# A router with stationary weights in four column groups, and attention's weighted values for two query blocks at once

## The chip, the cores and the metric

One core of a Trainium2 chip (trn2) runs one program. The metric is device time in microseconds (us) of one execution. The engines are TensorE (PE in the profile, its weight loads PEld), VectorE (DVE), ScalarE (ACT), GpSimd (POOL) and SyncE (SP, which here issues DMA transfers). Each engine works through its own instructions in order.

## The reference

An encoder of two layers on 512 tokens of 1024 values, float32. In each layer four mixers (Hyena, Mamba2, attention and HGRN2) work on 256 columns each, and an expert mixture follows. The change touches the weighting of values in attention (4 heads of 64) and the router.

```python
for l in range(DEPTH):                       # 2 layers
    hn = rmsnorm(x, norm_mix_w[l])
    proj = hn @ w_in[l]                      # columns for the four mixers
    ...
    x = x + concat([ya, yb, yc, yd]) @ w_out[l]
    x = x + expert_choice_moe(rmsnorm(x, norm_ffn_w[l]), ...)

def expert_choice_moe(x, w_router, w_gate, w_up, w_down):
    cap = EC_CAPACITY * L // N_EXPERTS       # 64 tokens for each of 16 experts
    aff = softmax(x @ w_router)              # 512 x 16
    gate, idx = top_k(swapaxes(aff, 1, 2), cap)
    xe = x[idx]
    hdn = silu(xe @ w_gate) * (xe @ w_up)
    ye = (hdn @ w_down) * gate
    ...
```

Attention's three bands come together in one table of biases that is added to the logits, so that the kernel makes, for each head, a softmax over 512 keys and the product with v.

## The kernel before, in words

A layer runs in stages: HGRN2, Mamba2, Hyena, attention, each woven with projections; then the router, then 16 experts. `weave` draws pieces from several streams by given shares and so fixes the order in which instructions are written. A framework keeps each engine's instructions in an order of its own making, close to it, and puts in the semaphores; the expert part keeps the order as written. Tiles come from pools of a fixed number of slots: N (9 slots), B (13), G (9 pages of 2 KB a partition, `page`), H (12) and others. A load into a slot waits until the slot's last reader is done.

Attention (`attn`) goes over two pairs of heads (i), four blocks of 128 queries (b) and the two heads of a pair (h). `logits` makes a 128x512 block of logits on PE (`alog`), adds the table and takes the maximum on DVE (L970), and the exponential and its sum on ACT (L973). `turn` follows three steps later: four PE transposes (`apT`), copied half by DVE (L982) and half by ACT (L983) into the page `aPT`. After the second head `weigh` multiplies with the values (`apv`, L990): for each of four key chunks and both heads a product into 64 of 128 partitions and 128 columns. After the last block of a pair `factors` and `values` scale it into `ars`, and it is split into a high and a low part (`mxh`, `mxl`) for the output projection. Attention is woven with that projection's other parts (`out_part`, tiles `po`, L1220 to L1222, each time three matmuls of 512 columns, added to x by DVE). A float32 matmul appears in the trace as two records for one instruction, a transpose as one.

The router (`router`) goes over four tiles of 128 tokens: eight transposes (`rxT`), copied by DVE and ACT (`rx`, L1273 and L1275), and eight matmuls `rl` (L1278) with a block of `rx` stationary (128x128) and 16 columns of the router's weights `rw` moving. DVE takes the maximum (L1280), ACT the sum of squares of the tile (`junk`, L1284, and `ssffn`) and the exponential (L1289). Then expert 0's affinities are laid out as rows (`er`), ranked on DVE (L1301), its tokens picked by matmuls (`ex`, L1335), transposed (`exT`), and the expert's three products follow (`eg`, `eu`, `ey`, L1399).

The experts' weights (`we`, L1391, 512 KB for a chunk of 128x1024) are loaded by SP into a ring of slots of the pools, as far ahead as slots come free. In attention and the router SP works through the loads for the first experts; behind them stand loads into slots that the experts themselves give back.

Of the kernel before, what the change touches and what calls it, by code (L numbers as in the profile page):

```python
# [15 lines left out]
AF = mybir.ActivationFunctionType  # L16
# [4 lines left out]
P = 128  # L21
# [3 lines left out]
NE = 16  # L25
# [7 lines left out]
R_NMIX, R_HCW, R_MCW, R_MCB, R_MNW, R_LB, R_HGN, R_FRQ, R_B1, R_B2, R_NFFN, R_N = (  # L33
    0, 8, 26, 46, 50, 52, 60, 61, 62, 63, 64, 72)

C_ID, C_LE, C_GE, C_IOTA, C_TOK, C_HALF, C_KEY, C_SLOT, C_N = 0, 128, 256, 384, 448, 452, 453, 455, 456


def shape_constants():
    f32 = np.float32  # L40
    p = np.arange(P)
    c = np.zeros((P, C_N), f32)
    c[:, C_ID:C_ID + P] = np.eye(P)
    c[:, C_LE:C_LE + P] = p[:, None] <= p[None, :]
    c[:, C_GE:C_GE + P] = p[:, None] >= p[None, :]
    c[:, C_IOTA:C_IOTA + 64] = np.arange(1, 65)
    c[:, C_TOK:C_TOK + 4] = 2 * (P * np.arange(4)[None, :] + p[:, None])
    c[:, C_HALF] = p >= 64
    c[:, C_KEY] = 1.0 / KEY
    c[:, C_KEY + 1] = 1.0  # L50
    c[:, C_SLOT] = p % 64 + 1
    same = (p[:, None] // 32) == (p[None, :] // 32)
    m = np.zeros((P, 2, P), np.int32)
    m[:, 0] = same & (p[:, None] <= p[None, :])
    m[:, 1] = same & (p[:, None] >= p[None, :])

    eo = np.concatenate([np.arange(0, L, 2), np.arange(1, L, 2)])
    f = 2.0 * np.pi * (np.arange(P, dtype=np.float64) + 0.5) / (2 * L)  # L60
    n = np.arange(L).reshape(P, 4).T
    th = n[:, :, None] * f
    dft = np.stack([np.cos(th), np.sin(th)]).astype(f32)
    idft = np.ascontiguousarray(dft.transpose(0, 1, 3, 2))
    tk = [eo[:, None] * f, eo[:, None] * (np.pi / 2 - f)]
    kdft = np.stack([np.concatenate([np.cos(tk[0]), np.cos(tk[1])], axis=1),
                     np.concatenate([np.sin(tk[0]), -np.sin(tk[1])], axis=1)])
    kdft = (kdft * (2.0 / (2 * L))).astype(f32)

    t = np.linspace(0.0, 1.0, L, dtype=f32)[:, None]  # L70
    ang_pos = (f32(2.0 * math.pi) * np.arange(L, dtype=f32) / f32(L)).astype(f32)
    bands = np.linspace(1e-4, 15, 16, dtype=f32)
    ang = (ang_pos[:, None] * bands[None, :]).astype(f32)
    z = np.concatenate([t, np.cos(ang), -np.sin(ang)], axis=-1).astype(f32)
    lo = math.log(1e-2) / 1.5
    hi = math.log(1e-2) / 0.3
    deltas = np.abs(np.linspace(lo, hi, 256, dtype=f32))
    decay = np.exp(-t * deltas[None, :]).astype(f32)[eo]

    d = np.arange(511, -512, -1)  # L80
    n = np.abs(d)
    nf = np.maximum(n, 1).astype(f32)
    large = 8 + (np.log(nf / f32(8)) / f32(math.log(128.0)) * f32(8)).astype(np.int32)
    bucket = (d > 0) * 16 + np.where(n < 8, n, np.minimum(large, 15))
    mult = (n <= 64).astype(int) + ((n <= 256) & (n % 4 == 0)) + (n % 16 == 0)
    oh = np.zeros((33, 1024), f32)
    oh[bucket, np.arange(1023)] = 1.0
    oh[32, :1023] = np.where(mult > 0, np.log(np.maximum(mult, 1)), -1e30)
    return {
        "c_pack": c, "c_hmask": m, "c_dft": dft, "c_idft": idft, "c_kdft": kdft,  # L90
        "c_zT": np.ascontiguousarray(z.T), "c_decay": decay, "c_bucket": oh,
    }
# [18 lines left out]
def encoder(ctx: ExitStack, tc: tile.TileContext, d, out, dbg=None, stages=None, nlayers=NL):  # L111
    nc = tc.nc
    V, A, G, T, SY = nc.vector, nc.scalar, nc.gpsimd, nc.tensor, nc.sync
# [24 lines left out]
    def tl(tag, shape, name, dt=F32):  # L138
        return tagged(pools[tag], tag, shape, dt, name)

    def small(shape, name, dt=F32, bufs=1):
        return tagged(sm, "s_" + name, shape, dt, name, bufs=bufs)
# [4 lines left out]
    def bank_b(name):  # L147
        return tagged(psb, "b", [512], F32, name)

    def page(shape, name, dt=F32):  # L150
        return tl("G", shape, name, dt)
# [52 lines left out]
    pk = cp.tile([P, C_N], F32, name="pk")  # L204
# [11 lines left out]
    def xrow(t):  # L216
        return X[t]
# [735 lines left out]
    def attn(l, st, scr, ahead=3):  # L953
        q, k, v = st
        mix_tile(2)
        tab, den, PT, po = {}, {}, {}, {}

        def logits(i, b, h):
            if b == 0 and h == 0:
                tab[i] = [tl("B", [896], "atab") for _ in range(2)]  # L960
                for g in range(2):
                    SY.dma_start(tab[i][g], bass.AP(tensor=scr.tensor, offset=scr.offset + (2 * i + g) * 1024,
                                                    ap=[[1, P], [1, 896]]))
                den[i] = small([4, 2], "aden", bufs=2)
            ps = bank_b("alog")
            for m in range(2):
                T.matmul(ps, q[i][:, h, b * P:(b + 1) * P], k[i][m][:, h], start=(m == 0), stop=(m == 1))
            lg = page([L], "alg")
            mx = small([1], "amx", bufs=4)
            V.tensor_tensor_reduce(lg, ps, tab[i][h][:, 128 * b:128 * b + 512][:, ::-1], 1.0, -3e38,  # L970
                                   ALU.add, ALU.max, mx)
            V.tensor_scalar(mx, mx, -1.0, None, op0=ALU.mult)
            A.activation(lg, lg, AF.Exp, bias=mx, accum_out=den[i][:, b, h:h + 1])  # L973
            return lg

        def turn(i, b, h, lg):
            pt = bank_b("apT")
            for c in range(4):
                T.transpose(pt[:, c * P:(c + 1) * P], lg[:, c * P:(c + 1) * P], ident)
            PT[h] = page([4, P], "aPT")  # L980
            src = pt.rearrange("p (c q) -> p c q", c=4)
            V.tensor_copy(PT[h][:, 0:2], src[:, 0:2])  # L982
            A.activation(PT[h][:, 2:4], src[:, 2:4], AF.Copy)  # L983

        def weigh(i, b):
            if b == 0:
                po[i] = bank_a("apv")
            for c in range(4):
                for g in range(2):
                    T.matmul(po[i][64 * g:64 * g + 64, b * P:(b + 1) * P],  # L990
                             v[:, c, (2 * i + g) * 64:(2 * i + g + 1) * 64], PT[g][:, c],
                             start=(c == 0), stop=(c == 3))

        def factors(i):
            V.reciprocal(den[i], den[i])
            dn = page([4, 2, 64], "adn")
            V.tensor_copy(dn, den[i][:, :, :, None].to_broadcast([P, 4, 2, 64]))
            pr = bank_b("aden")
            for b in range(4):
                T.transpose(pr[:, b * P:(b + 1) * P], dn[:, b].rearrange("p h c -> p (h c)"), ident)  # L1000
            rs = page([L], "ars")
            A.activation(rs, pr, AF.Copy)
            return rs

        def values(i, rs):
            V.tensor_mul(rs, rs, po[i])
            mix_put(2, i, rs)

        todo = [(i, b, h) for i in range(2) for b in range(4) for h in range(2)]
        lgs = {}  # L1010
        for n in range(len(todo) + ahead):
            if n < len(todo):
                lgs[n] = logits(*todo[n])
            m = n - ahead
            if m >= 0:
                turn(*todo[m], lgs.pop(m))
                end = todo[m][1:] == (3, 1)
                if end:
                    rs = factors(todo[m][0])
                if todo[m][2]:  # L1020
                    weigh(*todo[m][:2])
                if end:
                    values(todo[m][0], rs)
            yield 2
# [229 lines left out]
    def router(rw, st, xd):  # L1254


        pl = bank_b("rl")
        plv = pl[:, :64].rearrange("p (t e) -> p t e", t=4)
        rt = tl("H", [D], "ra")
        ra = rt[:, :12 * NE].rearrange("p (t e c) -> p t e c", t=4, e=NE)  # L1260
        mx = small([4], "rmx")
        den = small([4], "rden")
        V.tensor_copy(ra[:, :, :, 2], pk[:, C_TOK:C_TOK + 4, None].to_broadcast([P, 4, NE]))
        for t in range(4):
            xs = []
            for h in range(2):
                ps = bank_b("rxT")
                for k in range(4):
                    T.transpose(ps[:, k * P:(k + 1) * P], xrow(t)[:, (4 * h + k) * P:(4 * h + k + 1) * P], ident)
                xT = page([4, P], "rx")  # L1270
                src = ps.rearrange("p (k c) -> p k c", k=4)
                if not h:
                    V.tensor_copy(xT, src)  # L1273
                else:
                    A.activation(xT, src, AF.Copy)  # L1275
                xs.append(xT)
            for k in range(8):
                T.matmul(plv[:, t], xs[k // 4][:, k % 4], rw[:, k], start=(k == 0), stop=(k == 7))  # L1278
            af, r = ra[:, t, :, 0], ra[:, t, 0, 1:2]
            V.reduce_max(mx[:, t:t + 1], plv[:, t], axis=AX.X)  # L1280
            V.tensor_scalar(af, plv[:, t], mx[:, t:t + 1], None, op0=ALU.subtract)
# [353 lines left out]
```

## Time and profile before

| | us |
|---|---|
| runs of the kernel | 1667.71, 1661.7, 1661.99 (median 1661.99) |
| the profiled execution's own time | 1665.74 |
| its span in the trace | 1664.0 |
| TensorE busy in the span | 1536.9 (92%) |
| VectorE | 805.7 (48%) |
| ScalarE | 396.1 (24%) |
| moved by DMA | 468.55 MB, 282 GB/s over the span |

The span is from the first to the last instruction of the trace. A busy share is an average over stages: in the experts' stages TensorE and the DMA are both nearly always busy, in the mixers only TensorE. What bounds a stage has to be read in that stage.

### The profile page before, as it was taken

What the parts mean: (1) busy time and instruction counts of PE and PEld (TensorE: products, weight loads), DVE (VectorE), ACT (ScalarE), POOL (GpSimd) and SP (SyncE); (2) the same over time, 40 slices, a digit from 0 to 9 for tenths busy, and PEclk for the clock granted to TensorE, in tenths of its full rate; (3) what the DMA queues carried; (4) which work ended last, traced back from release to release, by engine and by line L of the source; (5) the groups of instructions that cost most, each with busy time, mean ns of one, the idle gap of its engine ahead of it and who ended that gap; (6) DMA issues with size and microseconds to landing.
All of it is one profiled execution on the core that took longest, in us unless ns stands there. A gap on an engine that the chain in (4) does not pass through costs nothing.

```text
span 1664.0 us, 22783 instructions
## 1 busy us (share of the span) xinstructions
PE 1536.9 (92%) x8899; PEld 879.6 (53%) x8899; DVE 805.7 (48%) x1727; ACT 396.1 (24%) x805; POOL 214.0 (13%) x214
## 2 busy tenths in 40 slices
PE   7989999989999998998889999999899999999985
PEld 6778788763433433332368788787534433332332
DVE  6777777562433342331266767856533433332323
ACT  4344434430001010000152435243200001000012
POOL 3232132000000000000033232300000000000001
PEclk9989999989999999999989889999899999999998
DMA  5411224679999999999912202167799999999995
GB/s 165 129 51 28 75 76 162 237 265 369 421 419 422 420 421 420 420 422 420 385 54 80 74 26 77 55 231 261 256 402 419 420 421 420 421 420 420 420 421 239
DMA packets 153486, 468.55 MB, mean 282 GB/s; under 512 B 20408, under 2 KB 56664, under 8 KB 144418
## 3 DMA queue, kind: packets, MB, share of 16 engines
q1 hardware_dynamic: 144742, 455.10, 69.8%
q0 software_dynamic: 2240, 7.34, 1.1%
q10 hardware_dynamic: 6396, 4.65, 0.8%
q8 instruction: 70, 1.15, 0.3%
q14 instruction: 38, 0.31, 0.0%
HBM read 460.60 MB, written 6.44 MB: 281 GB/s over the span
## 4 chain that ended last, share of the span: by engine, by line
PE 61%; DMA 25%; DVE 6%; ACT 3%; issue 2%; POOL 2%; ACTq 0%; SPq 0%; DVEq 0%; POOLq 0%
DMA we<-in_moe_w_up_dram 10%; PE eg L1399 9%; DMA we<-in_moe_w_down_dram 7%; PE eu L1399 7%; PE ey L1399 7%; DMA we<-in_moe_w_gate_dram 6%; PE pcm L395 3%; PE pcm L396 3%; PE pcm L397 3%; PE ec L1470 3%; PE po L1220 2%; PE po L1221 2%; PE po L1222 2%; PE ptm L418 2%; PE ptm L417 2%
## 5 line engine op out<-in xcount | busy, mean ns | idle before, releaser
L1399 PE MATMUL eu<-we,exT 128*64 128x512 f32 x1024 | 239.4, 599 | 20.3 <-DMA we<-in_moe_w_up_dram 18.4
L1399 PE MATMUL ey<-we,ehT 128*64 128x512 f32 x1024 | 232.9, 598 | 18.8 <-ACT ehT L1435 11.5
L1399 PE MATMUL eg<-we,exT 128*64 128x512 f32 x1024 | 231.2, 597 | 10.6 <-DMA we<-in_moe_w_gate_dram 5.9
L1399 PEld LDWEIGHTS eu<-we,exT 128*64 128x64 f32 x1024 | 67.0, 136 | 187.2 <-issue 87.9
L1301 DVE SCALAR_TENSOR_TENSOR ra<-er,ra,tie 128x512 bf16<-128x512 f32 x128 | 95.9, 749 | 135.4 <-PE er L1309 132.5
L1399 PEld LDWEIGHTS ey<-we,ehT 128*64 128x64 f32 x1024 | 69.0, 136 | 157.9 <-issue 96.3
L1399 PEld LDWEIGHTS eg<-we,exT 128*64 128x64 f32 x1024 | 68.8, 136 | 151.4 <-issue 107.3
L1452 DVE SCALAR_TENSOR_TENSOR eY<-ey,erg,eY 64x512 fp32r<-64x512 f32 x64 | 48.0, 749 | 205.3 <-ACT eY L1451 205.2
L1420 ACT ACTIVATE eh<-eg 128x512 f32<-128x512 f32 x32 | 19.1, 598 | 505.3 <-PE eg L1399 505.3
L397 PE MATMUL pcm<-hT,whl 128*128 128x512 f32 x320 | 128.9, 403 | 3.5 <-DVE whl L381 3.5
L396 PE MATMUL pcm<-hT,whl 128*128 128x512 f32 x320 | 130.3, 407 | 0.0
L395 PE MATMUL pcm<-hT,whl 128*128 128x512 f32 x320 | 130.1, 406 | 0.0
L1471 DVE TENSOR_TENSOR x<-x,ec 128x512 f32<-128x512 f32 x128 | 79.8, 682 | 102.8 <-PE ec L1470 102.8
L1346 POOL DMA_INDIRECT exe<-xd,erow x28 | 27.8, 994 | 783.2 <-DVE erg L1327 526.6
L1451 ACT ACTIVATE eY<-ey,erg 64x512 fp32r<-64x512 f32 x64 | 43.7, 683 | 269.4 <-PE ey L1399 245.0
L1427 DVE TENSOR_TENSOR eh<-eh,eu 128x512 f32<-128x512 f32 x32 | 22.0, 688 | 158.7 <-PE eu L1399 158.7
L417 PE MATMUL ptm<-wtm,hT 128*128 128x256 f32 (+1 forms) x256 | 76.5, 300 | 1.7 <-DVE aqs L924 1.7
L1470 PE MATMUL ec<-eY,eot 128*128 128x512 f32 x256 | 67.3, 405 | 10.2 <-DVE erow L1344 6.4
L418 PE MATMUL ptm<-wtm,hT 128*128 128x256 f32 (+1 forms) x256 | 74.6, 293 | 1.3 <-DVE wtm L381 1.3
L380 POOL TENSOR_SCALAR whl<-wraw 128x1024 fp32r<-128x1024 f32 x40 | 46.7, 1169 | 222.1 <-PE pcm L397 113.8
L419 PE MATMUL ptm<-wtm,hT 128*128 128x256 f32 (+1 forms) x256 | 73.7, 291 | 0.0
L397 PEld LDWEIGHTS pcm<-hT,whl 128*128 128x128 f32 x320 | 62.4, 195 | 18.3 <-DVE whl L381 3.9
(386 smaller groups left out, 2381.4 us busy)
## 6 DMA issues: line engine op xcount, KB each, us to landing
we<-in_moe_w_gate_dram SPq DMA_DIRECT2D x216, 512.0 KB
we<-in_moe_w_up_dram SPq DMA_DIRECT2D x208, 512.0 KB
we<-in_moe_w_down_dram SPq DMA_DIRECT2D x204, 512.0 KB
wraw<-in_w_in_dram SPq DMA_DIRECT2D x27, 1024.0 KB
we<-in_moe_w_down_dram SPq DMA_DIRECT2D x26, 1024.0 KB
we<-in_moe_w_up_dram SPq DMA_DIRECT2D x24, 1024.0 KB
we<-in_moe_w_gate_dram SPq DMA_DIRECT2D x20, 1024.0 KB
wo<-in_w_out_dram SPq DMA_DIRECT2D x8, 1024.0 KB
```

Source lines behind the costliest of these rows:

```text
L380: G.tensor_scalar(dst_hi, raw, 1.0, 0.0, op0=ALU.mult, op1=ALU.add)
L395: T.matmul(ps, w[:, 0, k, :], H[k], start=(k == 0), stop=False)
L396: T.matmul(ps, w[:, 0, k, :], Lo[k], start=False, stop=False)
L397: T.matmul(ps, w[:, 1, k, :], H[k], start=False, stop=(k == 7))
L417: T.matmul(dst, h, w[:, 0, k % 4], start=(k == 0), stop=False)
L418: T.matmul(dst, h, w[:, 1, k % 4], start=False, stop=False)
L419: T.matmul(dst, g, w[:, 0, k % 4], start=False, stop=(k == 7))
L1301: V.scalar_tensor_tensor(g, pr, ra[:, c, e, 0:1], tie[:, 384 - c * P:896 - c * P], op0=ALU.subtract, op1=ALU.is_gt, accum_out=k)
L1399: T.matmul(ps[f][64 * f:64 * f + 64], xT[:, j, h], qs[4 * h + j][:, f * 512:(f + 1) * 512], start=(h == 0 and j == 0), stop=(h == 1 and j ...
L1452: V.scalar_tensor_tensor(lo, src, w[c, 0:1], hi.bitcast(F32), op0=ALU.mult, op1=ALU.subtract)
L1470: T.matmul(ps, ot[:, t * P:(t + 1) * P], Y[i][q][n], start=(q == 0), stop=(q == 1))
L1471: V.tensor_add(xrow(t)[:, c], xrow(t)[:, c], ps)
```

## The change

Attention: the tile `aPT` now holds a head's transposed weights for two blocks of queries (4 chunks x 2 blocks x 128) and comes from pool N, where it came from the page pool for one block. `weigh` runs after every second block, with 256 moving columns where it had 128, so half as many instructions.

Router: the weights are padded with zeros to eight blocks of 128x32 (`rp`, in the tile `ra`) and are now the stationary side; the tokens (`rx`, 128 columns) move. Block k writes into the 32 output partitions of its column group k mod 4 (`rc`, L1285), so that four partial sums stand one below the other. DVE copies them to SBUF (`rpart`, L1288), and one matmul with a 0/1 matrix of 128x16 from the constants (`C_SUM`) as the moving side adds the four groups and gives the logits (`rl`, L1289). A PSUM bank more is used.

```diff
@@ shape_constants
+    c[:, C_SUM:C_SUM + NE] = (p % 32)[:, None] == np.arange(NE)
...
@@ attn
-            PT[h] = page([4, P], "aPT")
+            if b % 2 == 0:
+                PT[h] = tl("N", [4, 2, P], "aPT")
             src = pt.rearrange("p (c q) -> p c q", c=4)
-            V.tensor_copy(PT[h][:, 0:2], src[:, 0:2])
-            A.activation(PT[h][:, 2:4], src[:, 2:4], AF.Copy)
+            V.tensor_copy(PT[h][:, 0:2, b % 2], src[:, 0:2])
+            A.activation(PT[h][:, 2:4, b % 2], src[:, 2:4], AF.Copy)
 
         def weigh(i, b):
-            if b == 0:
+            if b == 1:
                 po[i] = bank_a("apv")
             for c in range(4):
                 for g in range(2):
-                    T.matmul(po[i][64 * g:64 * g + 64, b * P:(b + 1) * P],
-                             v[:, c, (2 * i + g) * 64:(2 * i + g + 1) * 64], PT[g][:, c],
+                    T.matmul(po[i][64 * g:64 * g + 64, (b - 1) * P:(b + 1) * P],
+                             v[:, c, (2 * i + g) * 64:(2 * i + g + 1) * 64], PT[g][:, c].rearrange("p b q -> p (b q)"),
                              start=(c == 0), stop=(c == 3))
...
-                if todo[m][2]:
+                if todo[m][1] % 2 and todo[m][2]:
                     weigh(*todo[m][:2])
...
@@ router
-        pl = bank_b("rl")
+        pc, pl = bank_b("rc"), bank_b("rl")
...
+        rp = rt[:, 768:].rearrange("p (k c) -> p k c", k=8)
+        V.memset(rp, 0.0)
+        V.tensor_copy(rp[:, :, :NE], rw)
...
             for k in range(8):
-                T.matmul(plv[:, t], xs[k // 4][:, k % 4], rw[:, k], start=(k == 0), stop=(k == 7))
+                q = k % 4
+                T.matmul(pc[32 * q:32 * q + 32, t * P:(t + 1) * P], rp[:, k], xs[k // 4][:, k % 4],
+                         start=(k < 4), stop=(k >= 4))
+            part = page([P], "rpart")
+            V.tensor_copy(part, pc[:, t * P:(t + 1) * P])
+            T.matmul(plv[:, t], part, pk[:, C_SUM:C_SUM + NE], start=True, stop=True)
```

The order of instructions differs in attention and the router of each layer. On TensorE, at layer 0's first weighing of values in attention, before (a name's number tells one tile from another; `aks` and `aqs` are keys and queries, `av` the values, `wos` the projection's weights):

```order
L967 MATMUL alog_2744<-aks_2414,aqs_2336 128x512
L990 MATMUL apv_2721<-aPT_2702,av_2481 64x128
L1220 MATMUL po_2730<-wos_2639,mxh_2179 128x512
L1221 MATMUL po_2730<-wos_2639,mxh_2179 128x512
L1222 MATMUL po_2730<-wos_2639,mxl_2180 128x512
L1220 MATMUL po_2730<-wos_2639,mxh_2179 128x512
L990 MATMUL apv_2721<-aPT_2718,av_2481 64x128
L990 MATMUL apv_2721<-aPT_2702,av_2481 64x128
L990 MATMUL apv_2721<-aPT_2718,av_2481 64x128
```

and at the first weighing after the change:

```order
L980 MATMUL apT_2758<-pk,alg_2692 128x128 x4
L968 MATMUL alog_2788<-aks_2414,aqs_2336 128x512
L992 MATMUL apv_2765<-aPT_2702,av_2481 64x256
L1222 MATMUL po_2774<-wos_2639,mxh_2179 128x512
L1223 MATMUL po_2774<-wos_2639,mxh_2179 128x512
L1224 MATMUL po_2774<-wos_2639,mxl_2180 128x512
L992 MATMUL apv_2765<-aPT_2718,av_2481 64x256
L992 MATMUL apv_2765<-aPT_2702,av_2481 64x256
L992 MATMUL apv_2765<-aPT_2718,av_2481 64x256
L992 MATMUL apv_2765<-aPT_2702,av_2481 64x256
L992 MATMUL apv_2765<-aPT_2718,av_2481 64x256
```

The first `apv` instruction still stands alone, with projection matmuls behind it, and the others follow; but this happens once for two blocks. Counted over a layer's attention, the `apv` instructions stand in 19 runs before and in 10 after (between the runs are other tiles' matmuls); 13 of the 19, and 7 of the 10, stand ahead of the last `alog`.

On TensorE, at the end of layer 0's router, where the last two tiles of tokens are worked on, before (`pk` holds the identity for transposes, `x_93` is the last tile of tokens):

```order
L1278 MATMUL rl_3225<-rw_471,rx_3339 128x16 x4
L1269 MATMUL rxT_3386<-pk,x_93 128x128 x4
L1278 MATMUL rl_3225<-rw_471,rx_3346 128x16 x4
L1269 MATMUL rxT_3393<-pk,x_93 128x128 x4
L1309 MATMUL er_3430<-pk,ra_3226 128x128
L1278 MATMUL rl_3225<-rw_471,rx_3391 128x16 x4
L1309 MATMUL er_3430<-pk,ra_3226 128x128
L1278 MATMUL rl_3225<-rw_471,rx_3398 128x16 x4
```

and after:

```order
L1274 MATMUL rxT_3365<-pk,x_93 128x128
L1285 MATMUL rc_3185<-rx_3315,ra_3187 32x128 x4
L1274 MATMUL rxT_3365<-pk,x_93 128x128 x3
L1320 MATMUL er_3405<-pk,ra_3187 128x128
L1289 MATMUL rl_3186<-pk,rpart_3325 128x16
L1285 MATMUL rc_3185<-rx_3363,ra_3187 32x128 x4
L1320 MATMUL er_3405<-pk,ra_3187 128x128
L1285 MATMUL rc_3185<-rx_3370,ra_3187 32x128 x4
L1289 MATMUL rl_3186<-pk,rpart_3380 128x16
```

Four `rl` instructions in a row became four `rc` in a row, and one product `rl` for each tile of tokens stands behind them, with the next tile's work between where there is any; behind the last `rc` nothing is left to stand between.

On SP, the last loads that are issued ahead of layer 0's experts, before. The tiles 3210 and 3212 are the last in this row of loads that reuse a slot of attention or its projection; 3667 waits for expert 0's matmuls:

```order
L1391 DMA we_3660<-in_moe_w_up_dram 128x2048
L1391 DMA we_3662<-in_moe_w_up_dram 128x1024
L1391 DMA we_3210<-in_moe_w_down_dram 128x1024
L1391 DMA we_3212<-in_moe_w_down_dram 128x1024
L1391 DMA we_3662<-in_moe_w_up_dram 128x1024
L1391 DMA we_3665<-in_moe_w_up_dram 128x2048
L1391 DMA we_3667<-in_moe_w_up_dram 128x1024
```

and after, where 3170 and 3172 are the last that reuse a slot of attention or its projection, and 3642 waits for expert 0's matmuls:

```order
L1402 DMA we_3170<-in_moe_w_down_dram 128x1024
L1402 DMA we_3172<-in_moe_w_down_dram 128x1024
L1402 DMA we_3598<-in_moe_w_down_dram 128x1024
L1402 DMA we_3598<-in_moe_w_up_dram 128x1024
L1402 DMA we_3635<-in_moe_w_up_dram 128x2048
L1402 DMA we_3637<-in_moe_w_up_dram 128x1024 x2
L1402 DMA we_3640<-in_moe_w_up_dram 128x2048
L1402 DMA we_3642<-in_moe_w_up_dram 128x1024
```

The loads behind the last reused slot became more: two N slots that took weights before are taken by `aPT`.

## Rows read from the trace of the kernel before

**Rows 1.** Windows: stretch, length, each engine's busy time, granted clock, DMA share, GB/s.
```profile
365.00:375.00 10.00, 9.02 (x48) 3.32 (x50) 7.79 (x28) 1.88 (x2) 0.00 (x0) 0.84 0.13 54
290.00:300.00 10.00, 10.00 (x62) 7.48 (x60) 4.87 (x15) 3.65 (x12) 0.00 (x0) 1.00 0.88 352
...
1550.00:1600.00 50.00, 44.10 (x212) 14.99 (x208) 10.63 (x24) 5.12 (x8) 2.38 (x3) 1.00 1.02 421
```

**Rows 2.** SP's queue on the timeline: start, length (waits included), issue.
```profile
354.99 19.85 SPq L1391 DMA_DIRECT2D we<-in_moe_w_up_dram  x3
375.38 10.97 SPq L1391 DMA_DIRECT2D we<-in_moe_w_gate_dram  x8
```

**Rows 3.** Chain of waits, layer 0's attention: start us, length, engine, tile, line.
```profile
293.22 0.36 PE apv L990 x2
293.58 0.43 PE po L1220
...
294.47 0.23 PE po L1220
294.71 1.02 PE apv L990 x14
...
339.40 0.80 PE apv L990 x10
```

**Rows 4.** Chain of waits: expert 0's first products.
```profile
373.40 7.09 PE eg L1399 x32
```

**Rows 5.** Timeline at the end of layer 0's attention.
```profile
332.24 0.42 DVE L982 COPY aPT<-apT 128x256 f32<-128x256 f32 x1
...
333.03 0.71 ACT L973 ACTIVATE alg<-alg,amx 128x512 f32<-128x512 f32 x1
...
333.64 0.19 ACT L973 ACTIVATION_READ_ACCUMULATOR alg<-alg,amx 128x1 f32 x1
...
343.16 0.30 PEld L1222 LDWEIGHTS po<-wos,mxl 128*128 128x128 f32 x2 [0.19 <-DVE mxl L461]
```

**Rows 6.** Chain of waits in layer 0's router, and one row of expert 0.
```profile
346.76 0.80 PE rl L1278 x8
...
357.00 1.02 PE rl L1278 x8
...
358.27 1.53 PE rl L1278 x8
...
380.49 0.41 PE ers L1322 x15
```

**Rows 7.** Timeline at the end of layer 0's router.
```profile
357.20 0.58 ACT L1275 ACTIVATE rx<-rxT 128x512 f32<-128x512 f32 x1
...
359.83 0.17 DVE L1280 TENSOR_REDUCE rmx<-rl 128x1 f32<-128x16 f32 x1 [1.71 <-PE rl L1278]
...
360.04 0.24 DVE L1281 TENSOR_SCALAR ra<-rl,rmx 128x16 f32<-128x16 f32 x1
...
361.16 0.16 DVE L1287 TENSOR_TENSOR ssffn<-ssffn 128x1 f32<-128x1 f32 x1 [0.17 <-ACT junk L1284]
```

**Rows 8.** Windows of 1 us around the router, layer 0 and layer 1.
```profile
358.00:359.00 1.00, 1.00 (x8) 1.00 (x6) 0.12 (x1) 0.47 (x2) 0.00 (x0) 0.50 0.99 332
368.00:369.00 1.00, 1.00 (x5) 0.13 (x2) 0.09 (x1) 0.00 (x0) 0.00 (x0) 0.91 0.00 0
1190.00:1191.00 1.00, 1.00 (x6) 0.27 (x4) 1.00 (x5) 0.00 (x0) 0.00 (x0) 0.61 0.00 0
```

**Rows 9.** Chain of waits: expert 0's gather, layer 0 and layer 1.
```profile
367.66 1.28 PE ex L1335 x4
...
369.30 1.89 PE ex L1335 x8
...
1186.92 1.91 PE ex L1335 x4
...
1189.45 2.58 PE ex L1335 x8
```

More of the change, by code (lines that the diff above doesn't have):

```diff
@@ L34 @@
     0, 8, 26, 46, 50, 52, 60, 61, 62, 63, 64, 72)
-C_ID, C_LE, C_GE, C_IOTA, C_TOK, C_HALF, C_KEY, C_SLOT, C_N = 0, 128, 256, 384, 448, 452, 453, 455, 456
+C_ID, C_LE, C_GE, C_IOTA, C_TOK, C_HALF, C_KEY, C_SLOT, C_SUM, C_N = 0, 128, 256, 384, 448, 452, 453, 455, 456, 472
 def shape_constants():
```

## The prediction

> **What bounds the kernel now.** I read the busy windows first. While experts run, the 16 DMA engines are saturated: 421 GB/s at a DMA share of 1.02 over 50 us of layer 1's experts, while TensorE is busy for 44.1 of them [rows 1]. So an expert stage takes the time of its bytes, and each layer ends a fixed time after its stream of expert weights restarts. The restart is in SP's queue: its last prefetches of "up" weights are followed by an issue that stands until the first `eg` matmul of expert 0 gives back a weight tile; the eight "gate" loads after it begin at 375.38 [rows 2]. Just before, between 365 and 375 us, the DMA share is 0.13 [rows 1]: the prefetch has filled every tile and the transfers lie idle for about 8.7 us. Whatever brings the first `eg` forward by d therefore shortens the layer by d, as long as the prefetch is still done before it.
>
> What sets the first `eg` is the chain of waits ahead of it. In attention the chain is TensorE alone: its busy time is 10.00 of 10 us in the window shown [rows 1]. Then come the router's logits, a short chain over DVE and ScalarE, and expert 0's rank and gather. The change touches attention and the router, in each of two layers.
>
> **Attention.** The chain shows the first weighing in pieces: two `apv` matmul records take 0.36 us, the projection's `po` behind them 0.43, a later `po` 0.23 to 0.24, and fourteen `apv` records 1.02 [rows 3]. Fourteen against two give (1.02 - 0.36)/12 = 0.055 us a record, so 0.25 us are paid to enter a run of `apv`, and 0.43 - 0.24 = 0.19 to leave it: 0.44 for every run of `apv` between others. In layer 0 the chain holds 19 such runs, from 293.22 to 339.40 (the shown ones are four of them), with 128 records in all. What the change halves is the count of records, not the columns: 64 records of 256 columns instead of 128 of 128. A 512-column record takes 7.09/32 = 0.22 us [rows 4], a 128-column one 0.055, so time goes by columns and 64 x 0.11 = 128 x 0.055 = 7.0 us: nothing is won there. What is won is runs: the changed order has 10 a layer instead of 19. If all nine count, that is 9 x 0.44 = 4.0 us a layer.
>
> I don't count all nine. Thirteen of the old runs lie before the last `alog`, seven of the new: 6 x 0.44 = 2.7 us, on an engine that is never idle there. I take 0.2 off, since at the second pair the matmuls wait for a DVE copy of `aPT` (0.42 us [rows 5]) which now has less cover. Behind the last `alog` six old runs stand against three new ones, but there the end isn't TensorE's: the last weights pass through the exponential on ScalarE (333.03 + 0.71 + 0.19 for its sum [rows 5]), and in the changed order the last `apT` stands ahead of the projection's next part, so that TensorE stops for some 0.7 us of the 3 x 0.44 = 1.3 saved. `ars`, `mxh` and `mxl` follow as before, and the `po` that waits for `mxl` at 343.16 [rows 5] comes 0.4 us earlier against the last `alog`. Sum: -(2.7 - 0.2 + 0.4) = **-2.9 us a layer**, at most -4.0.
>
> **Router.** Eight `rl` records take 0.80 us, 0.10 each, and there are eight such groups a layer; the last two, 1.02 and 1.53, run as the clock falls [rows 6]. New: eight groups of eight `rc` records, each to 32 output partitions and 128 columns wide. No row has that shape. From above, 0.055 a record (`apv`, 128 columns, if the four column groups take turns) or 0.107 (if in addition no weight load hides under another group's matmul); from below 0.41/15 = 0.027 (`ers`, three columns wide [rows 6]), if the groups overlap. With 0.25 to enter and 0.19 to leave, as `apv` pays, a group costs 0.66 to 0.88 against 0.80, so -1.1 to +0.6 a layer; I take the middle, -0.2, since the rows lie equally near. The four product matmuls `rl` add some 0.27 each (the fixed part of a run) and are issued where TensorE otherwise waits for `rx` copies, so I count one in four of them, +0.3.
>
> The end of the router is a chain. ScalarE copies the last half of x at 357.20 (0.58), the last `rl` follow at half clock, and DVE takes the maximum at 359.83 [rows 7]: 2.05 us from copy to maximum. After the change, in its place: one `er` (0.26), eight `rc` (0.69 at full clock, up to 1.1 at half), a hop, the DVE copy of 128x128 (0.42 for 256 columns [rows 5] and 0.24 for 16 [rows 7] give 0.32), a hop and the product (0.27): 1.7 to 2.2 with hops of 0.1. So -0.3 to +0.2; taken -0.1. Behind it nothing moves: exponential, `junk`, the sum of squares at 361.16, `er`. Router: -0.2 + 0.3 - 0.1 = **0**, with -0.6 and +0.7 as the ends, and +2.7 in the case of 0.107 (eight groups dearer by 0.42 are 3.3, less what lies in waits).
>
> What the Trainium skill says of this change, in TensorEngine Tiling (Array Packing), section Key Properties, is that a change of tiling mode drains TensorE; the 0.25 and 0.19 at the edges of `apv` agree with a drain, and by that page the router's eight new groups pay it too, as the sum has it.
>
> The two memsets and copies that build `rp`, 13 more DVE rows a program, lie in attention, where DVE works 4.87 of 10 us [rows 1]; the 16 more columns of `pk` ride on a load at the start: 0.
>
> **Prefetch.** `aPT` now holds two N tiles in attention that were free for weights, so SP issues them later. In the order, 5.0 MB of loads stand behind the last tile that attention or its projection gives back, instead of 2.5 to 3.0. At 0.42 MB/us [rows 1] they take 12 us; from about 349.5 they end near 365 with what is queued ahead, and the first `eg` would be wanted near 370.5. The 8.7 idle microseconds shrink to about 5; cost 0.
>
> **The clock.** In layer 0 the granted clock is 0.50 from 358 on and 0.91 by 368 to 369; in layer 1 it is still 0.61 thirteen microseconds after the fall, in 1190 to 1191 [rows 8]. The same `ex` matmuls cost 1.28 + 1.89 in layer 0 and 1.91 + 2.58 in layer 1 [rows 9]: 1.3 us for a late return. Which of the two a layer draws I can't derive; layer 1 can only gain and layer 0 only lose, and with the router's matmuls lighter, layer 0 is the likelier to change: half of 1.3, **+0.7**.
>
> **Sum.** 2 x (-2.9) + 0 + 0.7 = -5.1 us. The profiled execution took 1665.74 for a span of 1664.0; it would take 1660.6. The median of the runs shown is 1661.99, 3.75 below the profiled one, and gives **1657** (-0.3%). A half per cent, 8.3 us, is about what a measurement of this kernel can tell from no change.
>
> **Rivals.**
> - *The gain in full* (0.2). All nine runs count and `rc` overlaps: -(4.0 + 0.6) a layer, 1652.8, or 1651.5 with layer 1's clock back as early as layer 0's. For it: the chain is TensorE for 60 us. Against it: the exponential in the tail.
> - *No weight load hides under another group* (0.12): +2.7 a layer, 1657 + 5.4 = 1662.3; the router gives back what attention won. `rc` would show 0.107 a record.
> - *The router's matmuls go four times as fast* (0.06). Eight groups of 0.80 are 6.4 us; a quarter of that saves 4.8 a layer, so 1657 - 9.6 = 1647.4. Against it stand the fixed 0.44 a run and the chain of copy and product. This is the Trainium skill's TensorEngine Tiling (Array Packing), section Theoretical Speedup, up to four times for a dimension of at most 32; no row here shows groups of 32.
> - *Slower, by a late prefetch* (0.08). The 5 MB stand behind one `po`. If that `po`, or another tile in front, comes over 5 us later than I reckon, the last loads end after the first `eg`, and the restart gives nothing: each microsecond beyond costs one a layer. With ten late, 1657 + 2 x 5 = 1667; from 7.5 on it is slower than before. For it: SP waits in order. Against it: the 8.7 us.
> - *Nothing comes of it* (0.1): TensorE's time in attention is filled by waits for DVE and ScalarE, which no longer have its runs as cover; 1662.
> - The forecast itself has 0.44.
>
> The range goes from 1651.5 (the gain in full with the early clock) to 1663 (loads not hidden, clock late); outside lie the fourfold case and the late prefetch. Faster by over 0.5% means below 1653.7: the fourfold case, over half of the gain in full and a few hundredths of the forecast, 0.22. Slower by over 0.5%, above 1670.3: only a prefetch some 12 us late or the clock falling much earlier, 0.07. Within: 0.71.
>
> **What would show it.** Ten runs of `apv` a layer on the chain, each still 0.44 dearer than its columns; TensorE standing about 0.7 us for the last exponential; eight `rc` in 0.5 to 0.7 us; the sum of squares of the last tile about 3 us earlier in layer 0 and 6 in layer 1; the "gate x8" of SP at about 372 instead of 375.38, with idle DMA still ahead of it. It would be wrong if new waits stood in attention's chain, if `rc` took over 0.9 us, if the DMA were busy up to the first `eg`, or if 128 columns by two took less than 256 by one.

## The result, and the profile after

The changed kernel takes 1672.68 us in the median (1669.84 to 1680.41, 6 runs) against 1662.1 for the kernel before: a ratio of 1.0055, 95% interval [1.0035, 1.0075]. By that ratio it is slower by 9 us; the forecast was 5 us faster. The profiled execution took 1678.36 us, with a span of 1676.6.

**In attention and the router the change shortens the stages, as forecast.** The chain of waits after, in layer 0's attention (start, length, engine, tile, line), answers to [rows 3]:

```profile
301.69 0.57 PE apv L992 x2
302.26 0.43 PE po L1222
...
303.16 1.87 PE apv L992 x14
...
340.38 1.44 PE apv L992 x10
```

Twelve records more cost 1.87 - 0.57 = 1.30, so 0.108 us a record of 256 columns, twice the 0.055 of 128. To leave a run costs 0.43 - 0.24 = 0.19 as before (0.43 for the `po` behind it, 0.24 for a plain one). To enter one costs more than before: two records take 0.57, of which 0.22 are their columns, so 0.35 where runs of 128 columns paid 0.25. A run is now 0.54 us dearer than its columns, where it was 0.44. There are ten runs in the layer, from 301.69 to 340.38. The rows of `alog` and `rxT` in layer 0 (line, engine, operation, count: durations in ns, first and last start in us) give the stages' lengths, first for the kernel before:

```profile
L967 PE MATMUL alog<-aks,aqs x32: 389/394/486, 284.2 to 330.2; 128*128 128x512 f32 x32
...
L1269 PE MATMUL rxT<-pk,x x32: 271/273/307, 344.6 to 356.6; 128*128 128x128 f32 x32
```

and for the whole change in experiment e9 below (its line numbers differ by a few):

```profile
L967 PE MATMUL alog<-aks,aqs x32: 389/394/486, 287.7 to 331.5; 128*128 128x512 f32 x32
...
L1275 PE MATMUL rxT<-pk,x x32: 272/273/329, 345.8 to 356.7; 128*128 128x128 f32 x32
```

From the first to the last `alog` 46.0 us became 43.8, from there to the first `rxT` 14.4 became 14.3, from the first to the last `rxT` 12.0 became 10.9. In the changed kernel's own trace these are 43.8, 14.3 and 10.9. In layer 0, from the first `alog` to the first `eg` it is 373.4 - 284.2 = 89.2 before and 373.7 - 288.1 = 85.6 after; up to SP's "gate x8" in layer 1, with first `alog` at 1103.4 and 1110.1, it is 92.8 and 87.9. So 3.6 and 4.9 us are won in this pair of traces. The 4.9 is in part the trace of before, whose layer 1 is the longest of its kind: over the eight traces in which attention and the router are unchanged, the first `alog` to the first `eg` takes 88.4 to 90.8 us, on average 89.2 in layer 0 and 89.4 in layer 1; over the three with the whole change it is 85.4 and 86.1. That makes 3.8 and 3.3 us, 7.1 together.

**What lost more than that is the rate of the expert weights.** Windows after, in the middle of layer 1's experts (columns as in [rows 1]):

```profile
1300.00:1500.00 200.00, 185.99 (x982) 71.70 (x984) 67.28 (x158) 17.86 (x28) 11.76 (x14) 1.00 1.02 411
```

and the same window before:

```profile
1300.00:1500.00 200.00, 190.36 (x1014) 75.84 (x1012) 72.62 (x173) 17.93 (x28) 11.78 (x14) 1.00 1.02 420
```

The DMA share is 1.02 in both, so the DMA engines are as busy, but they move 411 GB/s instead of 420 for the same bytes, and TensorE waits more (185.99 against 190.36 us busy). It is so in layer 0 too, and in every saturated slice of the page. SP's queue after, which answers to [rows 2], with layer 1's restart added:

```profile
355.21 19.98 SPq L1402 DMA_DIRECT2D we<-in_moe_w_up_dram  x6
375.72 10.97 SPq L1402 DMA_DIRECT2D we<-in_moe_w_gate_dram  x8
...
1198.01 10.97 SPq L1402 DMA_DIRECT2D we<-in_moe_w_gate_dram  x8
```

From layer 1's restart to the end of the span it is 1676.6 - 1198.01 = 478.6 us; before, with the restart at 1196.20, it was 467.8: 10.8 us longer. In layer 0, from the first `eg` to layer 1's first copy of `gv` (860.5 before, 869.5 after) it is 495.8 against 487.1: 8.7 longer.

The ledger of the two profiled executions at the first `alog`, the first `eg` or restart, in each layer, and at the end of the span: +3.9, +0.3, +6.7, +1.8, +12.6. The first +3.9 isn't the change's: most of it arises long before attention. The first `fk` matmul, of the filters that Hyena uses, starts at 75.0 us before and at 77.9 after, and between 70 and 80 us the granted clock was 0.70 in this execution and 1.00 in the one before. Over all the traces below the first `alog` starts between 282.8 and 290.1 us, in kernels with the same work up to there; such an offset is no property of a kernel.

### The profile page after: what moved, and what is told of

Its sections match the earlier page's. It is cut to its first block, busy times and chain, and to the rows that moved or that the text cites. A ratio compares the mean times of both kernels' runs of the same rounds, so it can differ in the third digit from the quotient of the medians.

```text
span 1676.6 us, 22560 instructions
## 1 busy us (share of the span) xinstructions
PE 1535.4 (92%) x8787; PEld 858.4 (51%) x8787; DVE 808.4 (48%) x1739; ACT 395.5 (24%) x805; POOL 214.9 (13%) x214
## 4 chain that ended last, share of the span: by engine, by line
PE 59%; DMA 26%; DVE 8%; ACT 3%; issue 2%; POOL 1%; ACTq 0%; SPq 0%; DVEq 0%; POOLq 0%
DMA we<-in_moe_w_up_dram 9%; PE eg L1410 9%; DMA we<-in_moe_w_down_dram 9%; PE eu L1410 7%; PE ey L1410 7%; DMA we<-in_moe_w_gate_dram 5%; PE pcm L396 3%; PE pcm L398 3%; PE pcm L397 3%; PE ec L1481 3%; PE ptm L419 2%; PE ptm L418 2%; PE ptm L420 1%; PE po L1222 1%; PE po L1223 1%
## 5 line engine op out<-in xcount | busy, mean ns | idle before, releaser
L1410 PE MATMUL eu<-we,exT 128*64 128x512 f32 x1024 | 242.9, 601 | 27.8 <-DMA we<-in_moe_w_up_dram 27.1
L1462 ACT ACTIVATE eY<-ey,erg 64x512 fp32r<-64x512 f32 x64 | 43.7, 683 | 275.8 <-PE ey L1410 251.5
```

Source lines behind the costliest of these rows:

```text
L1410: T.matmul(ps[f][64 * f:64 * f + 64], xT[:, j, h], qs[4 * h + j][:, f * 512:(f + 1) * 512], start=(h == 0 and j == 0), stop=(h == 1 and j ...
```

## The experiments

What differs between the kernels in the experts' stage? The order as written is the same there, but the addresses are not. The constants' tile `pk` stands ahead of all pools in SBUF, and it grew from 456 to 472 columns, 64 bytes a partition. By the programs' memory layout the weight slots start at 27392 bytes and so on before, all multiples of 256, and at 27456 and so on after, all 64 past one. Three theories were set against each other. ADDRESS: the start of a slot within SBUF sets the rate. HBM: the constants' tensor, 8 KB longer, moves the weights in HBM. ORDER: the loads' new order and `aPT` in pool N.

**e1, the whole change with slots on multiples of 256.**

```diff
-    pk = cp.tile([P, C_N], F32, name="pk")
+    pk = cp.tile([P, C_N + 48], F32, name="pk")
...
-            SY.dma_start(pk, d["c_pack"])
+            SY.dma_start(pk[:, :C_N], d["c_pack"])
```

> The change with the SBUF tile of the constants 48 columns wider (unused), so that every weight slot behind it starts at a multiple of 256 bytes, as in the kernel before (27648, before 27392, changed kernel 27456). In the changed kernel's trace the saturated stretches move 410 GB/s where before moved 420. Theory ADDRESS (the slots' start within SBUF sets the transfer rate): 420 GB/s again, and the time is the changed kernel's less about 10 us a layer: 1652 to 1656. Theory HBM (the longer constants tensor moves the weights in HBM) and theory ORDER (the new order of loads and slots): 410 GB/s and 1670 to 1675.

1650.36 us (1649.65 to 1653.01), ratio to before 0.9925 [0.9898, 0.9953]. Its window:

```profile
1300.00:1500.00 200.00, 189.11 (x1016) 75.17 (x1013) 70.15 (x165) 17.91 (x28) 12.48 (x15) 1.00 1.02 420
```

The rate is back with the longer HBM tensor and the new order still there. The time is 22 us below the changed kernel's, and just under 2 below the lower end of what was expected.

**e2, the kernel before with 64 bytes more in the constants' tile** (`C_N + 16` in the same two lines).

> The kernel before with the SBUF tile of the constants 16 columns (64 bytes) wider, unused, and nothing else. Theory ADDRESS: saturated stretches at 410 GB/s, some 10 us more a layer, 1678 to 1684. Theories HBM and ORDER: 420 GB/s and 1662.

1686.64 us (1684.08 to 1688.51), ratio 1.0142 [1.0114, 1.017]. Its window:

```profile
1300.00:1500.00 200.00, 186.37 (x985) 71.78 (x982) 65.57 (x156) 17.92 (x28) 12.57 (x15) 1.00 1.02 410
```

Sixteen unused columns slow an otherwise unchanged kernel by 1.4%, a little more than expected. ADDRESS stands.

**e3, the kernel before with the longer tensor in HBM alone.**

```diff
-    c = np.zeros((P, C_N), f32)
+    c = np.zeros((P, C_N + 16), f32)
...
-            SY.dma_start(pk, d["c_pack"])
+            SY.dma_start(pk, d["c_pack"][:, :C_N])
```

> The kernel before with the constants' tensor in HBM 16 columns longer in each row (128x472), of which 456 are loaded; SBUF as before. Theory HBM: 410 GB/s, 1678 to 1684. Theories ADDRESS and ORDER: 420 GB/s and 1662.

1661.93 us (1658.35 to 1670.01), ratio 0.9994 [0.9976, 1.0013], and its window:

```profile
1300.00:1500.00 200.00, 190.38 (x1014) 75.71 (x1010) 71.15 (x164) 19.27 (x30) 11.77 (x14) 1.00 1.02 420
```

HBM falls.

**e4, the attention part alone**, with `pk` as before: the diff's lines in `turn`, `weigh` and the loop.

> The attention part of the change alone: constants, router and slots' addresses as before. Theory ORDER: 410 GB/s and slower than before, about 1670. Theories ADDRESS and HBM: 420 GB/s, and the gain of attention alone, 2.9 us a layer by the prediction's sum (at most 4.0): 1654 to 1658.

1659.36 us (1651.17 to 1663.01), ratio 0.996 [0.994, 0.9981], 421 GB/s between 500 and 550 us. ORDER falls. The time is just above the expected 1654 to 1658. From the first to the last `alog` it takes 43.7 us (290.1 to 333.8).

**e5, the router part alone**, with the constants' tile 520 columns wide as in e1.

> The router part of the change alone (attention as before), with the constants' tile 520 columns wide so that weight slots start at multiples of 256 bytes. Saturated stretches at 420 GB/s. If the prediction's zero for the router holds: 1662 (-0.6 to +0.7 a layer). The trace of the change with its slots moved back to multiples of 256 bytes shows eight `rc` records in 0.35 us where the prediction had 0.5 to 0.7, so theory OVERLAP (the four column groups work at the same time): 1 to 2.5 us a layer less, and up to 1.3 more where the clock falls or returns at another time: 1655 to 1660.

1661.09 us (1656.28 to 1665.57), ratio 0.9987 [0.9969, 1.0005]: no difference that the timing can tell. The stage does get shorter: first to last `rxT` 343.2 to 354.1, 10.9 us against 12.0. So OVERLAP is borne out by the `rc` matmuls' 0.35 us, but of its 1 to 2.5 us a layer only the lower end came, and the time lies above its 1655 to 1660, for the reasons in the next section.

**e6, e7 and e8, the kernel before with 32, 128 and 256 bytes more** (`C_N + 8`, `+ 32`, `+ 64`).

> The kernel before with the constants' tile 8 columns (32 bytes) wider: slots start 32 bytes past a multiple of 256. Theory GRID (any start off the grid costs the same piece more for every 4096-byte row): 410 GB/s, 1683 to 1688. Theory BYTES (the cost grows with the bytes from the grid line to the start): about half of what 64 bytes cost, 415 GB/s, some 1672 to 1675. The Trainium skill, DMA: Bandwidth & Descriptors, section How a descriptor splits into AXI transactions, speaks for BYTES: it counts 32-byte beats from the 256-byte boundary below the start, 129 against 128 here, which is an estimate of 0.8%.

> The kernel before with the constants' tile 32 columns (128 bytes) wider: slots start 128 bytes past a multiple of 256, on a multiple of 128. Theory GRID with a grid of 256: 410 GB/s, 1683 to 1688. Theory GRID with a grid of 128: 421 GB/s, 1662. Theory BYTES: twice what 64 bytes cost, 400 GB/s, some 1705 to 1710. By the same section of the Trainium skill it would be 132 beats against 128, an estimate of 3%.

> The kernel before with the constants' tile 64 columns (256 bytes) wider: slots start at multiples of 256 again, at other addresses. All theories on the start's remainder: 421 GB/s and the time of the kernel before, 1658 to 1665. If a wider tile or a shifted address by itself cost something: slower.

| bytes past a multiple of 256 | GB/s, 1300 to 1500 us | median us | ratio to before, interval |
|---|---|---|---|
| 32 (e6) | 410 | 1690.13 | 1.0169 [1.0146, 1.0192] |
| 64 (e2) | 410 | 1686.64 | 1.0142 [1.0114, 1.017] |
| 128 (e7) | 411 | 1681.32 | 1.0132 [1.0093, 1.0172] |
| 0, at 27648 (e8) | 420 | 1665.68 | 1.0012 [0.9997, 1.0028] |

The windows of e7 and of e8:

```profile
1300.00:1500.00 200.00, 187.10 (x988) 72.20 (x986) 67.31 (x158) 17.90 (x28) 11.76 (x14) 1.00 1.02 411
...
1300.00:1500.00 200.00, 190.69 (x1018) 76.26 (x1016) 70.31 (x163) 18.61 (x29) 11.76 (x14) 1.00 1.02 420
```

GRID with a grid of 256 bytes holds: 32, 64 and 128 past cost about the same, with times up to some 2 us outside the expected 1683 to 1688 on either side. A coarser grid is out too: 27392 is an odd multiple of 256 and 27648 a multiple of 512, and both are fast. BYTES falls, since 128 should have cost four times as much as 32. The Trainium skill, DMA: Bandwidth & Descriptors, section How a descriptor splits into AXI transactions, has the same grid: a transaction must start at a multiple of 256 bytes. The section words this for reads, while here the written side was shifted. An estimate from its count of beats, 129, 130 and 132 for a row of 4096 bytes against 128, would be 0.8, 1.6 and 3.1%, where the windows show 2.2 to 2.4% each time. The grid agrees with the measurement, the size doesn't follow that count. What a start off the grid does inside a transfer no run here shows.

**e9, the whole change at the addresses of the kernel before.** The 0/1 matrix is made on chip, so `pk` keeps its 456 columns:

```diff
+        su = rt[:, 208:208 + NE]
+        V.tensor_reduce(su, ident.rearrange("p (q c) -> p c q", q=4)[:, :NE], op=ALU.add, axis=AX.X)
...
-            T.matmul(plv[:, t], part, pk[:, C_SUM:C_SUM + NE], start=True, stop=True)
+            T.matmul(plv[:, t], part, su, start=True, stop=True)
```

> The whole change, but the 0/1 matrix that adds the four groups is made on chip, by one DVE sum over the identity's four groups of columns, in 16 free columns of the tile `ra`; the constants keep their 456 columns in HBM and SBUF, so every address is that of the kernel before. Theory ADDRESS: 421 GB/s and the time of the change with slots at multiples of 256 bytes, 1648 to 1655, 0.6 to 0.9% faster than before. If a wider constants' tile had helped by something else than its address: slower than that. From the stages' times (alog to first eg 85.3 to 86.1 us in place of 88.4 to 90.8) some 7 us are to be had: 1655 or a little below.

1650.03 us (1649.24 to 1655.49), ratio 0.9922 [0.9905, 0.9939], 421 GB/s. This version and e1 are faster than the kernel before by some 0.8%, and than the changed kernel by 1.3%.

**e10 and e12, half of the slots shifted.** In e10 an unused tile of 64 bytes stands between the pools N and B; in e12 the constants' tile is 64 bytes longer and 192 bytes stand there.

> The kernel before with an unused tile of 64 bytes between the pools N and B: the weight slots of H and N start at multiples of 256 bytes, those of B, W and S 64 bytes past. By the slots' sizes and uses 11.5 of 19.5 MB of a turn of the ring go to shifted slots, 59%. Theory ADDRESS, slot by slot: 0.41 at 421 and 0.59 at 410.5 GB/s make 415, and 0.59 of the 22 to 28 us: 1675 to 1679. If any shifted slot slows the whole stream: 410 GB/s, 1684 to 1688. If it isn't the slots' start but the constants' tile: 421 GB/s, 1662.

> The other half: the kernel before with the slots of H and N 64 bytes past a multiple of 256 and those of B, W and S on it (constants' tile 16 columns wider, an unused tile of 192 bytes between N and B); 41% of the ring's bytes go to shifted slots. With the first half shifted (59%) the rate was 418 GB/s and the time 6 us above before, a quarter of what all slots cost. If each slot has its own price and H and N are the dear ones: the rest of the 24 us, 412 to 413 GB/s and 1680. If the price rises faster than the share of shifted slots, whichever they are (shifted transfers hide behind unshifted ones while there are enough): 418 to 420 GB/s and 1664 to 1670.

e10: 1670.4 us (1664.23 to 1674.06), ratio 1.0037 [1.0024, 1.0051], 418 GB/s:

```profile
1300.00:1500.00 200.00, 189.57 (x1008) 74.99 (x1006) 70.90 (x168) 17.93 (x28) 11.78 (x14) 1.00 1.02 418
```

e12: 1666.21 us (1657.96 to 1670.03), ratio 1.0012 [0.9993, 1.0032], 420 GB/s. With 59% of the bytes in shifted slots a quarter of the price is paid, with 41% nothing that can be told. So "slot by slot" was wrong: the price rises faster than the share, and the two halves together cost 0.5% where all slots cost 1.4%. That shifted transfers hide behind others in flight would explain it, but that was only argued.

**e11, attention alone, `pk` 520 columns wide.**

> The attention part alone once more, with the constants' tile 64 columns wider, so slots at multiples of 256 at the same addresses as in the whole change with its slots moved back. Attention's part of the gain: two times 2.3 us (46.0 to 43.75 from the first to the last `alog`) and what the clock makes of it: 1655 to 1660. If the shifted addresses of that kernel, and not the router, gave it its lead over attention alone, then 1650 to 1653.

1656.55 us (1654.68 to 1657.08), ratio 0.9953 [0.9937, 0.9969]. With e4 that makes 0.4 to 0.5% for attention alone. The higher addresses by themselves give nothing: the 1650 to 1653 of that case did not come.

## Why the prediction was wrong

**The step that failed** is the half sentence on the constants: "the 16 more columns of `pk` ride on a load at the start: 0". As a load they cost nothing. But they shift every slot behind them, and the prediction took the experts' stage as "the time of its bytes" at a rate that stays. The rate fell from 420 to 411 GB/s. A layer's expert weights are 16 x 3 matrices of 1024x1024 float32, 201 MB: 479 us at 420 and 490 at 411, 10.5 us a layer by that estimate, where the two layers showed 8.7 and 10.8. No rival had it; the one on the slower side (a late prefetch) was another mechanism, and it didn't happen: SP's last loads are issued in time, and the DMA stood idle again ahead of the first `eg`, as the window shows:

```profile
370.00:375.00 5.00, 4.08 (x34) 1.87 (x32) 4.03 (x14) 1.88 (x2) 0.00 (x0) 1.00 0.12 51
```

Where [rows 1] had 8.7 idle us up to 375, a share of 0.12 leaves 4.4 of these 5; to the restart at 375.72 it is about 5, as forecast.

**Attention: right in kind, a little too large.** Forecast was 2.7 - 0.2 = 2.5 us up to the last `alog`; 2.2 to 2.3 came (46.0 to 43.7 or 43.8, both layers, in every trace with this part). The term that was mis-sized is the entry of a run, taken as 0.25 whatever its columns: with the 0.35 measured at 256 columns, thirteen old runs at 0.44 against seven new at 0.54 would save 1.9, not 2.7, as an estimate. The 0.4 behind it did not come (14.4 to 14.3). TensorE does stand there for the last exponential, 0.60 us where 0.7 were forecast. The timeline after:

```profile
334.85 0.71 ACT L974 ACTIVATE alg<-alg,amx 128x512 f32<-128x512 f32 x1
...
335.70 0.33 PE L980 MATMUL apT<-pk,alg 128*128 128x128 f32 x1 [0.60 <-ACT alg L974]
```

**Router: zero was too little, by about a microsecond a layer.** The chain after, which answers to [rows 6]:

```profile
348.40 0.35 PE rc L1285 x8
348.76 0.43 PE po L1224
...
358.92 0.40 PE rc L1285 x8
359.34 0.30 DVE rpart L1288
359.69 0.41 PE rl L1289 x2
```

Eight `rc` take 0.35 with 0.19 to leave (0.43 against 0.24): 0.54 where the forecast had 0.66 to 0.88 and the old `rl` 0.80. The copy `rpart` is 0.30 (forecast 0.32), the product 0.41 (0.27). So -0.26 eight times is -2.1, and the products and their copies, 0.13 to 0.41 and 0.20 to 0.30 where they stand on the chain, give much of it back; what is left at the last `rxT` is -1.1. The rival of matmuls four times as fast would have had 0.20 in place of the old 0.80; 0.35 came, between that and the forecast's 0.5 to 0.7, and the time did not follow, for the reason given against it: the run's edges and the chain behind it.

**Clock: another way than forecast.** Windows of 1 us after, which answer to [rows 8]:

```profile
358.00:359.00 1.00, 0.73 (x16) 0.34 (x17) 0.79 (x5) 0.81 (x5) 0.00 (x0) 1.00 0.99 389
...
363.00:364.00 1.00, 0.21 (x1) 0.00 (x0) 0.75 (x2) 0.00 (x0) 0.00 (x0) 0.50 0.86 348
...
368.00:369.00 1.00, 1.00 (x5) 0.06 (x2) 0.00 (x0) 0.00 (x0) 0.00 (x0) 0.50 1.08 451
```

The forecast had layer 0 lose 1.3 us in half of the cases by a late return. Now the whole router runs at 1.00, and the clock falls only after TensorE has stood nearly idle behind the last product; it returns late, as forecast. The chain's `ex` pieces show the late return:

```profile
367.10 1.91 PE ex L1346 x4
...
369.63 1.91 PE ex L1346 x8
```

Against layer 0's 1.28 + 1.89 in [rows 9] that is 0.65 more, and against the half-clock `rl` of 1.53 in [rows 6] some 0.7 less in the router, so the two nearly cancel. In layer 1 the `ex` pieces take 1.91 + 2.22 where [rows 9] have 1.91 + 2.58: 0.4 less.

**The sum without the address.** From `alog` to `eg` the stages say -7.1 us over all traces (-8.5 by the one pair); forecast were -5.1. Timed, e1 and e9 are 12 to 13 us below the kernel before (10 to 16 by e9's interval), attention alone 6.6 and 7.8, the router alone 2. So the forecast was too small here as well: 1650 lies just below its range. Some 5 of the 12 to 13 us are not placed in attention or the router: executions differ by 7 us before the first `alog` alone, so the few traces can't show them. That stays open.

## What to carry to other kernels

A tile that grows by a few bytes moves every tile behind it. Where a stage is bound by DMA into SBUF, keep the slots' start on a multiple of 256 bytes, and compare the GB/s of a saturated window before and after any change of layout: at the same DMA share of 1.02 it fell by 2.3% and cost more than the change gained. Runs of matmuls, not columns, were what the pairing of query blocks saved: each time TensorE turned to outputs of 64 partitions and back cost 0.44 us with 128 moving columns and 0.54 with 256.

## What the runs showed that I had not expected

Slots 32, 64 or 128 bytes past a multiple of 256 cost 22 to 28 us here by the ratios (1.3 to 1.7%), almost whatever the offset; with 41% of the bytes in such slots the cost could not be told from none, with 59% it was 0.4%.

Column groups of 32 and of 64 behaved differently here. Two groups of 64 gained nothing over the full width: `apv` takes 0.108 us a record of 256 columns and `eg` 0.22 of 512, where a `po` record of full width takes 0.23 for its 512 [rows 3]. Eight `rc` records of 128 columns on four groups of 32 take 0.35 us with the entry, less than the 8 x 0.055 = 0.44 that they would take in turn without any entry. If they pay the entry of 0.25 as `apv` does at 128 columns, 0.0125 a record is left, a quarter of 0.055; whether that is how it divides was not measured.
